# The RWKV stage of a decoder layer: elementwise work of POOL is given to DVE

## The chip, the cores and the metric

The kernel runs on one core of a Trainium2 chip. The metric is the device time of one execution in microseconds, as the median of several runs. Before the change it was 2909.91 us (three runs, 2908.15 to 2915.07).

The core's engines are named as the profile names them: PE (TensorE, matrix products; PEld is its weight load), DVE (VectorE), ACT (ScalarE), POOL (GpSimd) and SP (SyncE, which here issues the DMA transfers). Each works through its own queue in order and waits for the others by semaphores.

## The reference

One layer of a hybrid decoder, float32, on x of 1 x 1024 x 1024:

```
x <- x + 1/2 swiglu(rms_norm(x))
h  = rms_norm(x);  p = h @ w_in     -> RWKV columns | attention q, k, v | gates
y_a = rwkv7_time_mix(p_rwkv);  y_b = dilated_attention(q, k, v)
x <- x + (sigmoid(g_a) * (y_a @ w_proj_rwkv) + sigmoid(g_b) * (y_b @ w_proj_attn)) @ w_out
x <- x + 1/2 swiglu(rms_norm(x))
```

The part that matters here is the time mixing, with 16 heads of width 64:

```
r, k, v, ... = token_shift(p);  decay = exp(-exp(w));  a = sigmoid(...);  g = sigmoid(gd) @ g2
kk = heads(k * k_k);  kk = kk / max(sqrt(sum(kk * kk)), 1e-12)
k  = k * (1 + (a - 1) * k_a)
state_t = state * decay + (state @ -kk) (kk * a)^T + v k^T;   wkv_t = state_t @ r
y = (wkv - mean) * rsqrt(var + eps) * ln_w + ln_b
result = (y + sum(r * k * r_k) * v) * g
```

## The kernel before

All matrix products are float32 made of three products of high and low parts (`hi*hi + lo*hi + hi*lo`): ACT writes the high part, another engine subtracts it from the source to make the low part. The layer is a row of stages: a feed-forward half step, the attention with the projection of its columns, the RWKV stage with the rest of the projection, the output products, and a second half step.

The RWKV stage works on 8 pairs of heads (128 rows, `NP = 8`), each in two halves of 512 tokens: 16 units, numbered n. A half has 8 chunks (`HC`) of 64 tokens. For each unit four Python generators emit its instructions: `prep(n)` makes the decay products, kk, the scaled operands AL and BK and the masked chunk products Lab and MB; `solve(n)` inverts the triangular matrix of each chunk by five doubling steps (`pt` on PE, the masked B on DVE, `px` on PE, the sum XX and its transpose on DVE) and builds the chunk matrices M; `late(n)` transposes and makes the bonus; `chain(n)` carries the state SV through the 8 chunks and then normalises the output `o`, transposes it and writes y to the DRAM tensor `ya_d`.

Beside them runs the projection, `Dense.stream`: weight tiles of 128 columns, each loaded (`load`), split into `whi` and `wlo` (`parts`, lines 583 to 589) and multiplied by both halves of `hT` (`steps`, line 607, 24 products of 128x512 for a tile and a half of hT). Its products are what PE does while the solve waits. For a pair it makes k, r, v and mostly one gate tile. `db` is a second stream of that kind, for the attention's own projection with 768 rows, near the end of the stage.

The order comes from three layers. Each generator yields due times in units; `slotted` rounds those of the units down to sixteenths (`SLOTS = 16`); `drive` merges all generators by due time. That order is the priority with which the framework's scheduler then lays out each engine's queue, by its own costs of instructions, so that neighbours in a queue need not be neighbours in the code. In a queue the order is fixed. A tile pool with `bufs=n` hands a tag's buffer on when all uses of the tile that held it are done.

The lines that the change touches: line 588 (the low part of a weight tile: POOL where `pool_lo` is true, its default, which the attention stage uses as well), line 825 (`head_sum`: the low part `sl` for a sum over the rows of a head, called by `prep` for kk and by `late` for the bonus), lines 858 and 859 (the reciprocal of the root of kk, then its bound by 1e12), line 882 (r times the decay, the third part of AL), and lines 1096 to 1105 (the transposes of `o`, scale and shift by ln_w and ln_b on ACT out of PSUM, then bonus and gate on POOL). Others named later: L914 (`k2` times r_k and r, for the bonus), L669 (the carry of the token shift, one column), L876 (k's factor), L983, L985, L993 and L995 (B, the first XX, the later XX, the transpose of XX), L1048 to L1050 (M), L958 (the bonus itself, two buffers).

Of the kernel before, what the change touches and what calls it, by code (L numbers as in the profile page):

```python
# [9 lines left out]
AF = mybir.ActivationFunctionType  # L10
ALU = mybir.AluOpType
# [11 lines left out]
def f32(ap):  # L23
    return ap.bitcast(F32)
# [68 lines left out]
class Seven:  # L93
# [9 lines left out]
    def prep(self, j, n, k, lo, hi):  # L103

        nc, V = self.tc.nc, self.tc.nc.vector
        i = self.order[n]
        a11, a21, b11, b12 = lo
        a12, a22, b21, b22 = hi
        a, b = ((a11, b11), (a12, b21), (a11, b22), (a11, b11), (a21, b12), (a12, b22), (a22, b21))[i]
        ops = self.ring(j)  # L110
        split(nc, ops[0], ops[1], a)
        split(nc, ops[2], ops[3], b)
        self.b.append(ops)
        if i == 0:
            V.tensor_add(a21, a21, a22)
            V.tensor_sub(b12, b12, b11)
        elif i == 1:
            V.tensor_sub(a11, a21, a11)
            V.tensor_sub(a12, a12, a11)
        elif i == 5:  # L120
            V.tensor_sub(b22, b22, b12)
        elif i == 2:
            V.tensor_sub(a11, a22, a11)
            V.tensor_sub(b11, b22, b11)
        elif i == 3:
            V.tensor_sub(b21, b21, b22)
# [372 lines left out]
C = 64  # L499
# [67 lines left out]
class Dense:  # L567
# [15 lines left out]
    def parts(self, raw, n):  # L583
        nc, pool, kd = self.tc.nc, self.pool, self.kd
        whi = pool.tile([P, KD, P], F32R, tag="whi", name="whi", bufs=self.nw)
        wlo = pool.tile([P, KD, P], F32R, tag="wlo", name="wlo", bufs=self.nw)
        nc.scalar.copy(whi[:, :kd, :n], raw[:, :kd, :n])  # L587
        (nc.gpsimd if self.pool_lo else nc.vector).tensor_sub(wlo[:, :kd, :n], raw[:, :kd, :n], f32(whi[:, :kd, :n]))  # L588
        return whi, wlo

    def weights(self, c0, n=P):
# [84 lines left out]
SLOTS = 16  # L676
# [5 lines left out]
class Loras:  # L682
# [8 lines left out]
    def new(self, tag, shape, bufs=1, dt=F32):  # L691
        return self.pool.tile(shape, dt, tag="l_" + tag, name="l_" + tag, bufs=bufs)
# [92 lines left out]
class Rwkv:  # L785
# [34 lines left out]
    def head_sum(self, ps, src):  # L820

        nc, K = self.tc.nc, self.cx.K
        full, hi = src
        lo = self.new("sl", [P, HS], 1, F32R)
        nc.gpsimd.tensor_sub(lo, full, f32(hi))
        nc.tensor.matmul(ps, K["bones_r"], hi, start=True, stop=False)
        nc.tensor.matmul(ps, K["bones_r"], lo, start=False, stop=True)

    def prep(self, n):
        nc, cx, K, new = self.tc.nc, self.cx, self.cx.K, self.new  # L830
        p, half = n // 2, n % 2
        q, u = self.pairs[p], self.units[n]
        V, G = nc.vector, nc.gpsimd
        col = lambda name: K[name][:, p:p + 1]
        t0 = half * HS
        ts_ = slice(t0, t0 + HS)
        ch = lambda t: t.rearrange("p (c t) -> p c t", t=C)
        E, O = slice(0, 64), slice(64, 128)
        T = n - 2
        rows = slice(p * P, (p + 1) * P)  # L840
        at = lambda slot: T + slot / SLOTS
        yield at(-7)

        k = q.k[:, ts_]
        sq = new("sq", [P, HS])
        nc.scalar.activation(sq, k, AF.Square, scale=col("k_k"))
        hi = new("sh", [P, HS], 1, F32R)
        V.tensor_copy(hi, sq)
        pn = cx.ps_s.tile([P, 512], F32, tag="ps", name="pn")
        self.head_sum(pn, (sq, hi))  # L850
        kk = new("kk", [P, HS])
        nc.scalar.activation(kk, pn, AF.Sqrt)
        yield at(-6)
        tw, ta = new("tw", [P, HS]), new("ta", [P, HS])
        nc.sync.dma_start(tw, self.w_d[rows, ts_])
        nc.sync.dma_start(ta, self.a_d[rows, ts_])
        yield at(-4)
        V.reciprocal(kk, kk)
        G.tensor_scalar(kk, kk, 1e12, None, ALU.min)
        yield at(-3)  # L860
        V.tensor_tensor_scan(tw, K["reset"], tw, 0.0, ALU.mult, ALU.add)
        yield at(-1)
        lam = new("lam", [P, HC, C + 1])
        G.memset(lam[:, :, 0:1], 1.0)
        nc.scalar.activation(lam[:, :, 1:C + 1], ch(tw), AF.Exp, scale=-0.5 * E05)
        u.lamC = new("lamC", [P, HC, 1], 3)
        G.tensor_copy(u.lamC, lam[:, :, C:C + 1])
        nc.scalar.activation(tw, tw, AF.Exp, scale=0.5 * E05)
        inv = ch(tw)
        r = q.r[:, ts_]  # L870

        u.AL = AL = new("AL", [P, HC, 3, C], 2)
        yield at(1)
        V.scalar_tensor_tensor(kk, k, col("k_k"), kk, ALU.mult, ALU.mult)
        u.k2 = k2 = new("k2", [P, HS], 2)
        V.tensor_scalar(k2, ta, col("k_a"), col("c1"), ALU.mult, ALU.add)  # L876
        yield at(2)
        V.tensor_mul(k2, k2, k)
        V.tensor_mul(ta, ta, kk)
        BK = u.BK = new("BK", [P, HC, 2, C])  # L880
        yield at(4)
        G.tensor_mul(AL[:, :, 2], ch(r), lam[:, :, 1:C + 1])
        for b, h in enumerate((E, O)):
            yield at(4 + 2 * b)
            V.scalar_tensor_tensor(AL[h, :, b], ch(kk)[h], -1.0, lam[h, :, 0:C], ALU.mult, ALU.mult)
            V.tensor_mul(BK[h, :, b], ch(ta)[h], inv[h])
            yield at(5 + 2 * b)
            V.tensor_mul(BK[h, :, 1 - b], ch(k2)[h], inv[h])

        u.Lab = Lab = new("Lab", [P, HC, C], 2)  # L890
        u.MB = MB = new("MB", [P, HC, 2, P], 2)
        ms = lambda h: K["ms"][h].unsqueeze(1).broadcast_to([64, 4, C])

        def keep(x, base):
            G.affine_select(x, x, pattern=[[0, 4], [1, C]], compare_op=ALU.is_ge, fill=0.0, base=base, channel_multiplier=-1)
        for c0 in range(0, HC, 4):
            yield at(8 + c0 // 2)
            c4 = slice(c0, c0 + 4)
            heads = (E, O), (O, E)
            ps2 = [cx.ps_s.tile([P, 4, P], F32, tag="ps", name="plm") for _ in heads]  # L900
            for c in range(4):

                for e, (h, _) in enumerate(heads):
                    nc.tensor.matmul(ps2[e][:, c], BK[h, c0 + c].rearrange("p a b -> p (a b)"), AL[h, c0 + c, e:3:2 - e],
                                     start=True, stop=True)
            for e, (h, o) in enumerate(heads):
                ps = ps2[e]
                V.tensor_mul(Lab[h, c4], ps[h, :, 0:64], ms(h))
                nc.scalar.copy(AL[o, c4, e], ps[o, :, 0:64])
                nc.scalar.copy(MB[:, c4, e, self.TC[e]], ps[:, :, 64:128])  # L910
                keep(AL[o, c4, e], -1)
            if c0 == 0:
                yield at(9)
                V.scalar_tensor_tensor(k2, k2, col("r_k"), r, ALU.mult, ALU.mult)  # L914
        yield at(12)
        for e in range(2):
            for h in (E, O):
                for c0 in range(0, HC, 4):
                    keep(MB[h, c0:c0 + 4, e, self.TC[e]], 0)
# [132 lines left out]
    def chain(self, n):  # L1052
        nc, cx, K, new = self.tc.nc, self.cx, self.cx.K, self.new
        half = n % 2
        u = self.units[n]
        V = nc.vector
        yield n
        SV, lam = u.SV, u.lamC
        E, O = slice(0, 64), slice(64, 128)
        o = new("o", [P, 8, C])  # L1060
        for c in range(HC):
# [10 lines left out]
            if i == 3:  # L1072

                for par, dst in enumerate((E, O)):
                    for e, src in enumerate((O, E)):
                        k = slice(c - 3 + e, c + 1, 2)
# [3 lines left out]
        p = n // 2  # L1080
        col = lambda name: K[name][:, p:p + 1]
        ts_ = slice(half * HS, half * HS + HS)
        g = new("g", [P, HS])
        nc.sync.dma_start(g, self.g_d[p * P:(p + 1) * P, ts_])
        T = n + 1
# [7 lines left out]
        yield T + 0.20  # L1093
        V.reciprocal(st, st)
        V.tensor_mul(o, o, st.unsqueeze(2).broadcast_to([P, 8, C]))
        yield T + 0.27
        pt = cx.ps_s.tile([P, 4, P], F32, tag="ps", name="pyt")
        of = o.rearrange("p (i h) e -> p i (h e)", h=2)
        for c in range(4):
            nc.tensor.transpose(pt[:, c], of[:, c], cx.ident)  # L1100
        y = new("y", [P, HS])
        nc.scalar.activation(y, pt.rearrange("p a b -> p (a b)"), AF.Identity, bias=col("ln_b"), scale=col("ln_w"))
        yield T + 0.34
        nc.gpsimd.tensor_add(y, y, u.bonus)
        nc.gpsimd.tensor_mul(y, y, g)
        nc.sync.dma_start(self.y_d[p * P:(p + 1) * P, ts_], y)

    def run(self, gates, after):
# [335 lines left out]
def layer(tc, W, out):  # L1444
    nc = tc.nc
    cx = Ctx()
    with tc.tile_pool(name="const", bufs=1, reuse_waits="tile") as cp, tc.tile_pool(name="hT", bufs=1, reuse_waits="tile") as hp, \
# [3 lines left out]
        hT = fresh(F32R)  # L1451
# [24 lines left out]
        with ExitStack() as mix, ExitStack() as lt:  # L1476
# [70 lines left out]
            ps = lambda name, b: late.enter_context(pd(name, b))  # L1547
            cx.ps_s, cx.ps_c = ps("rs", 4), ps("rc", 2)
            rps = ExitStack()
            rw = Rwkv(tc, cx, dn, rps.enter_context(sb("rw")), rp2, dram, w_d, a_d, g_d, ya_d)  # L1550
            db = Dense(tc, cx, wp, hT, W["w_proj_attn"])

            def bring(t):
                yield t
# [22 lines left out]
            yp, y, w = None, [], []  # L1577
# [17 lines left out]
            wp = ws.enter_context(sb("w2"))  # L1595
# [6 lines left out]
        with os:  # L1602
# [4 lines left out]
            with ys, ws:  # L1607
# [6 lines left out]
                V = nc.vector  # L1614
# [125 lines left out]
```

## Time and profile before

| | before |
|---|---|
| median of three runs | 2909.91 us |
| the profiled execution | 2910.36 us, span 2908.6 us |
| PE busy | 2791.0 us, 96% |
| DVE busy | 2064.0 us, 71% |
| ACT busy | 1272.3 us, 44% |
| POOL busy | 738.9 us, 25% |
| RWKV stage | about 1140 to 2036 us of the span |

Busy time is the sum of an engine's instructions over the span. PE is busy nearly throughout; its products also take longer when the granted clock is low, so a busy PE need not be at its peak. The share of an engine over the whole span is an average over stages that have different limits.

### The profile page before, as it was taken

Reading aid. Unit: us, or ns where it says so; the run is one execution under the profiler, and the core shown is the slowest. Engines: PE = TensorE matmul, PEld = TensorE weight load, DVE = VectorE, ACT = ScalarE, POOL = GpSimd, SP = SyncE. Lnnn points to the kernel's source line nnn. Section 1 sums busy time; section 2 is a strip of 40 time slices with the busy share of each in tenths; the row PEclk is TensorE's granted clock in tenths of the full one; section 3 lists DMA queues with packets and bytes.
Section 4 is the critical chain, followed back from the end, with each engine's and each line's share of the span. In section 5 each row is a group of like instructions: output and inputs, shape, how many; then the busy total and the mean of one; then the engine's idle time right before and its main releaser. Section 6 shows DMA issues by size and latency. Waiting matters only on the chain. (4 is left out here: it accounts for less than half of the span.)

```text
span 2908.6 us, 56533 instructions
## 1 busy us (share of the span) xinstructions
PE 2791.0 (96%) x23406; PEld 2233.6 (77%) x23406; DVE 2064.0 (71%) x3058; ACT 1272.3 (44%) x2480; POOL 738.9 (25%) x739
## 2 busy tenths in 40 slices
PE   7999999998999999999999999999988999999999
PEld 5888887886667778777787777787767788887887
DVE  8666778997565763667666766624799777667998
ACT  5323332444566663455555556443435333233342
POOL 3332330001111112444343434322001333322000
PEclk9999999999999999999999999999999999999999
DMA  3222226103431123111111121128520122224221
GB/s 116 73 80 87 73 83 242 67 14 99 139 103 37 31 81 122 52 54 38 61 45 61 38 60 32 57 65 272 200 94 17 64 75 84 81 87 172 97 80 58
DMA packets 252242, 246.71 MB, mean 85 GB/s; under 512 B 26288, under 2 KB 192336, under 8 KB 251984
## 3 DMA queue, kind: packets, MB, share of 16 engines
q1 hardware_dynamic: 250832, 238.89, 25.2%
q8 instruction: 184, 3.01, 0.4%
q10 hardware_dynamic: 1152, 4.19, 0.4%
q14 instruction: 74, 0.61, 0.1%
HBM read 181.03 MB, written 62.01 MB: 84 GB/s over the span
## 5 line engine op out<-in xcount | busy, mean ns | idle before, releaser
L607 PE MATMUL pd<-hhi,whi 128*128 128x512 f32 (+1 forms) x1064 | 432.3, 406 | 5.2 <-DVE gb L1589 3.2
L607 PE MATMUL pd<-hlo,whi 128*128 128x512 f32 (+1 forms) x1064 | 436.1, 410 | 0.0
L607 PE MATMUL pd<-hhi,wlo 128*128 128x512 f32 (+1 forms) x1064 | 431.5, 406 | 0.6 <-POOL wlo L588 0.6
L282 PE MATMUL pp<-e,bh 128*128 128x512 f32 x1056 | 336.8, 399 | 3.9 <-ACT bh L74 2.3
L588 POOL TENSOR_TENSOR wlo<-raw,whi 128x1024 fp32r<-128x1024 f32 (+2 forms) x69 | 161.6, 2342 | 549.1 <-ACT whi L587 397.9
L282 PE MATMUL pp<-hhi,bl 128*128 128x512 f32 x704 | 276.4, 393 | 2.4 <-DVE bl L75 2.4
L282 PE MATMUL pp<-hhi,bh 128*128 128x512 f32 x704 | 277.3, 394 | 0.0
L282 PE MATMUL pp<-hlo,bh 128*128 128x512 f32 x704 | 276.1, 392 | 0.0
L74 ACT CAST bh<-rg 128x512 fp32r<-128x512 f32 x176 | 105.5, 621 | 344.4 <-DMA rg<-in_ffn_w_in_dram 172.3
L253 POOL TENSOR_TENSOR rg<-ru,rg 128x512 f32<-128x512 f32 x44 | 58.6, 1331 | 760.1 <-DVE bl L75 760.1
L607 PEld LDWEIGHTS pd<-hhi,whi 128*128 128x128 f32 (+1 forms) x1064 | 200.8, 189 | 52.4 <-issue 4.8
L282 PEld LDWEIGHTS pp<-e,bh 128*128 128x128 f32 x1056 | 200.0, 190 | 53.1 <-ACT bh L74 3.2
L607 PEld LDWEIGHTS pd<-hlo,whi 128*128 128x128 f32 (+1 forms) x1064 | 200.5, 188 | 48.0 <-issue 5.0
L607 PEld LDWEIGHTS pd<-hhi,wlo 128*128 128x128 f32 (+1 forms) x1064 | 200.9, 189 | 46.5 <-issue 4.8
L282 PE MATMUL pp<-e,bl 128*128 128x512 f32 x528 | 210.8, 399 | 0.0
L75 DVE TENSOR_TENSOR bl<-rg,bh 128x512 fp32r<-128x512 f32 x176 | 154.6, 879 | 73.8 <-ACT bh L74 73.8
L306 DVE TENSOR_TENSOR sg<-sg,pp 128x512 f32<-128x512 f32 x162 | 110.7, 683 | 102.3 <-PE pp L282 102.1
L282 PEld LDWEIGHTS pp<-hhi,bl 128*128 128x128 f32 x704 | 132.4, 188 | 33.3 <-DVE bl L75 3.3
L282 PEld LDWEIGHTS pp<-hlo,bh 128*128 128x128 f32 x704 | 132.3, 188 | 29.8
L282 PEld LDWEIGHTS pp<-hhi,bh 128*128 128x128 f32 x704 | 132.3, 188 | 29.3
L587 ACT CAST whi<-raw 128x1024 fp32r<-128x1024 f32 (+2 forms) x69 | 70.0, 1015 | 128.0 <-PE pd L607 72.0
L1071 ACT ACTIVATE SV<-pc,lamC 64x64 f32<-64x64 f32 x240 | 73.9, 308 | 113.8 <-PE pc L1068 111.6
(473 smaller groups left out, 6291.4 us busy)
## 6 DMA issues: line engine op xcount, KB each, us to landing
raw<-in_w_in_dram SPq DMA_DIRECT2D x60, 512.0 KB
rg<-in_ffn_w_in_dram SPq DMA_DIRECT2D x44, 512.0 KB
ru<-in_ffn_w_in_dram SPq DMA_DIRECT2D x44, 512.0 KB
act_d<-spill SPq DMA_DIRECT2D x80, 256.0 KB
e<-act_d SPq DMA_DIRECT2D x20, 512.0 KB
e<-in_ffn_w_out_dram SPq DMA_DIRECT2D x20, 512.0 KB
gt_d<-gate SPq DMA_DIRECT2D x32, 256.0 KB
x<-in_x_dram SPq DMA_DIRECT2D x8, 512.0 KB
```

Source lines behind the costliest of these rows:

```text
L74: nc.scalar.copy(hi, src)
L75: (eng or nc.vector).tensor_sub(lo, src, f32(hi))
L253: G.tensor_sub(b11, b12, b11)
L282: nc.tensor.matmul(ps, a[:, k], b[:, k], start=m == 0, stop=m == 11)
L306: add = lambda o, a: V.tensor_add(o, a, ps)
L587: nc.scalar.copy(whi[:, :kd, :n], raw[:, :kd, :n])
L588: (nc.gpsimd if self.pool_lo else nc.vector).tensor_sub(wlo[:, :kd, :n], raw[:, :kd, :n], f32(whi[:, :kd, :n]))
L607: nc.tensor.matmul(ps[:n], a[:, k, :n], b[:, k, t], start=i == 0, stop=i == 3 * kd - 1)
L1071: nc.scalar.activation(nxt[h, e], pc[h, i, e], AF.Copy, scale=lam[h, c])
```

## The change

DVE takes over POOL's work with two-dimensional tiles in the RWKV stage:

- The low part of a weight tile is made by DVE in pieces of four blocks of 128 columns (two for a tile) where `pool_lo` is false; that is set for the projection from the RWKV stage on, and for `db`.
- The rest `sl` of the sums over heads is made by DVE.
- kk is bounded from below by 1e-12 by DVE ahead of its reciprocal; before, the reciprocal was bounded from above by 1e12 by POOL.
- r times the decay is made by DVE.
- y: one DVE instruction takes the transposed output from PSUM, multiplies by ln_w and adds the bonus; a second adds ln_b and multiplies by the gate. ACT's instruction and POOL's two are gone. The transposes are due in slot 6 (before: 4), the last instruction in slot 7 (before: 5).

```
--- before.py
+++ after.py
@@ -585,7 +585,12 @@
         nc.scalar.copy(whi[:, :kd, :n], raw[:, :kd, :n])
-        (nc.gpsimd if self.pool_lo else nc.vector).tensor_sub(wlo[:, :kd, :n], raw[:, :kd, :n], f32(whi[:, :kd, :n]))
+        if self.pool_lo:
+            nc.gpsimd.tensor_sub(wlo[:, :kd, :n], raw[:, :kd, :n], f32(whi[:, :kd, :n]))
+        else:
+            for k in range(0, kd, 4):
+                k = slice(k, min(k + 4, kd))
+                nc.vector.tensor_sub(wlo[:, k, :n], raw[:, k, :n], f32(whi[:, k, :n]))
@@ -822,7 +827,7 @@
-        nc.gpsimd.tensor_sub(lo, full, f32(hi))
+        nc.vector.tensor_sub(lo, full, f32(hi))
@@ -855,8 +860,8 @@
         yield at(-4)
+        V.tensor_scalar(kk, kk, 1e-12, None, ALU.max)
         V.reciprocal(kk, kk)
-        G.tensor_scalar(kk, kk, 1e12, None, ALU.min)
@@ -879,7 +884,7 @@
         yield at(4)
-        G.tensor_mul(AL[:, :, 2], ch(r), lam[:, :, 1:C + 1])
+        V.tensor_mul(AL[:, :, 2], ch(r), lam[:, :, 1:C + 1])
@@ -1093,16 +1098,15 @@
-        yield T + 0.27
+        yield T + 6 / SLOTS
         pt = cx.ps_s.tile([P, 4, P], F32, tag="ps", name="pyt")
...
         y = new("y", [P, HS])
-        nc.scalar.activation(y, pt.rearrange("p a b -> p (a b)"), AF.Identity, bias=col("ln_b"), scale=col("ln_w"))
-        yield T + 0.34
-        nc.gpsimd.tensor_add(y, y, u.bonus)
-        nc.gpsimd.tensor_mul(y, y, g)
+        V.scalar_tensor_tensor(y, pt.rearrange("p a b -> p (a b)"), col("ln_w"), u.bonus, ALU.mult, ALU.add)
+        yield T + 7 / SLOTS
+        V.scalar_tensor_tensor(y, y, col("ln_b"), g, ALU.add, ALU.mult)
         nc.sync.dma_start(self.y_d[p * P:(p + 1) * P, ts_], y)
@@ -1547,8 +1551,9 @@
+            dn.pool_lo = False
             rw = Rwkv(tc, cx, dn, rps.enter_context(sb("rw")), rp2, dram, w_d, a_d, g_d, ya_d)
-            db = Dense(tc, cx, wp, hT, W["w_proj_attn"])
+            db = Dense(tc, cx, wp, hT, W["w_proj_attn"], pool_lo=False)
```

## Rows read from the trace of the kernel before

**Rows 1.** Windows: stretch, us, busy us of PE, PEld, DVE, ACT, POOL, clock, DMA.
```profile
1140.00:2036.00 896.00, 851.86 (x14748) 696.24 (x14747) 550.90 (x908) 458.26 (x1007) 354.71 (x475) 0.98 0.22 70
...
1326.00:1352.00 26.00, 20.95 (x580) 16.91 (x578) 20.45 (x34) 11.02 (x25) 7.49 (x6) 0.87 0.20 63
1426.00:1452.00 26.00, 21.68 (x597) 17.56 (x596) 21.48 (x37) 11.22 (x25) 7.49 (x6) 0.93 0.20 64
1525.00:1551.00 26.00, 21.66 (x596) 17.54 (x596) 21.29 (x37) 11.01 (x25) 7.49 (x6) 0.93 0.21 64
1623.00:1649.00 26.00, 20.56 (x596) 16.89 (x596) 21.43 (x37) 11.25 (x25) 7.48 (x6) 1.00 0.20 64
1721.00:1747.00 26.00, 21.79 (x592) 17.79 (x592) 21.06 (x35) 11.02 (x24) 7.48 (x6) 0.87 0.21 63
1819.00:1845.00 26.00, 22.53 (x586) 17.88 (x588) 17.63 (x30) 9.69 (x22) 7.04 (x11) 0.74 0.20 63
...
1367.00:1390.00 23.00, 22.92 (x379) 18.96 (x376) 17.32 (x33) 13.01 (x28) 5.51 (x8) 1.00 0.19 59
```

**Rows 2.** Waits in 1140 to 2036: total us, times, longest us.
```profile
PE pt L980 <- DVE XX L993: 15.6, 8, 2.3
PE px L991 <- DVE B L983: 7.6, 10, 1.2
PE pt L980 <- DVE M L1050: 5.8, 5, 1.2
...
DVE kk L874 <- POOL kk L859: 14.6, 15, 1.5
```

**Rows 3.** Timeline of DVE in an odd unit: start us, us, instruction.
```profile
1329.09 1.15 DVE L985 TENSOR_TENSOR XX<-B,eye 128x256 f32<-128x256 f32 x1
...
1335.26 2.75 DVE L914 SCALAR_TENSOR_TENSOR k<-k,v_r_k,r 128x512 f32<-128x512 f32 x1
...
1338.59 0.89 DVE L669 TENSOR_TENSOR r<-r,carry 128x1 f32<-128x1 f32 x1
1339.40 0.41 DVE L993 TENSOR_TENSOR XX<-XX,px 128x256 f32<-128x256 f32 x1
1339.73 1.36 DVE L876 TENSOR_SCALAR k<-ta,v_k_a,c 128x512 f32<-128x512 f32 x1
...
1343.05 0.41 DVE L983 TENSOR_TENSOR B<-pt,mk 128x256 f32<-128x256 f32 x1
```

**Rows 4.** Timeline of POOL in the same stretch, with its idle time before.
```profile
1328.78 1.19 POOL L882 TENSOR_TENSOR AL<-r,lam 128x512 f32<-128x512 f32 x1 [10.14 <-DVE M L1050]
...
1335.09 2.37 POOL L588 TENSOR_TENSOR wlo<-raw,whi 128x1024 fp32r<-128x1024 f32 x1 [1.18 <-ACT whi L587]
...
1339.54 1.26 POOL L1105 TENSOR_TENSOR y<-y,g 128x512 f32<-128x512 f32 x1
```

**Rows 5.** Single lines of code: count: ns least/median/most, first and last start.
```profile
L914 DVE SCALAR_TENSOR_TENSOR k<-k,v_r_k,r x16: 750/753/2748, 1155.5 to 1869.2; 128x512 f32<-128x512 f32 x16
...
L669 DVE TENSOR_TENSOR k<-k,carry x8: 148/150/153, 1150.7 to 1793.0; 128x1 f32<-128x1 f32 x8
...
L669 DVE TENSOR_TENSOR v<-v,carry x8: 1037/1047/1185, 1172.2 to 1861.6; 128x1 f32<-128x1 f32 x8
...
L876 DVE TENSOR_SCALAR k<-ta,v_k_a,c x16: 523/1182/1686, 1148.7 to 1827.5; 128x512 f32<-128x512 f32 x16
...
L75 DVE TENSOR_TENSOR ring<-y,ring x28: 678/688/708, 2029.6 to 2137.7; 128x512 fp32r<-128x512 f32 x28
```

**Rows 6.** Groups of POOL in 1140 to 2036: busy us, mean ns, idle before.
```profile
L588 POOL TENSOR_TENSOR wlo<-raw,whi 128x1024 fp32r<-128x1024 f32 (+1 forms) x43 | 99.1, 2305 | 95.4 <-ACT whi L587 77.9 <-PE pd L607 11.7 <-DVE gb L1589 5.7
```

**Rows 7.** Timeline of an even unit: DVE's first XX, PE's use of it.
```profile
1376.07 0.41 DVE L985 TENSOR_TENSOR XX<-B,eye 128x256 f32<-128x256 f32 x1
...
1377.69 0.75 PE L980 MATMUL pt<-XX,Lab 32*32 32x32 f32 x64
```

## The prediction

> **What bounds the kernel now.** I read the page first: TensorE is the busiest engine by far, so a change is worth only what it takes out of TensorE's idle time and out of its slow-clock time. The edits touch one stage, the RWKV stage, so next came the windows of that stage. In them the reader is to see [rows 1] that in 896 us TensorE is busy 851.9, idle 44.1, at a mean granted clock of 0.98. DVE is busy 551 us, 61%, POOL 355: by the average DVE is far from a bound. The windows by stretch show that the loss is local. In six stretches of 26 us, one in nearly every pair of heads, TensorE idles 5.05, 4.32, 4.34, 5.44, 4.21 and 3.47 us, 26.8 together, and there the granted clock falls to 0.87, 0.93, 0.93, 1.00, 0.87 and 0.74: weighted by length 17.2 us, an upper bound of what the low level (1.2 in place of 2.4 GHz) costs. The stretch between two of them (1367 to 1390) has TensorE busy 22.92 of 23 us. I call the units with a loss odd, the others even.
>
> Third, the waits of TensorE [rows 2]: it waits for DVE, in the triangular solve. `pt` waits for the sum XX (8 times, 15.6 us, longest 2.3), `px` for the masked B (10 times, 7.6), the first `pt` of a unit for the adds of M (5 times, 5.8). A separate row is DVE's own wait for POOL at kk, 14.6 us over 15 times.
>
> Fourth, the DVE queue inside one of the stretches [rows 3], beside POOL's [rows 4]. DVE is full there, and some of its instructions are far too long: L985 takes 1.15 us, 0.41 in an even unit [rows 7]; L914 2.75 against a median of 0.753 [rows 5]; L669, one column, 0.89 against 0.15 [rows 5]; L876 1.36 against 0.523 at best [rows 5]. Each of these runs while POOL works: L882 from 1328.78 to 1329.97, L588 from 1335.09 to 1337.46, L1105 from 1339.54 to 1340.80. L914 starts 0.17 after L588 and ends at 1338.01, 0.55 after it: it stood until POOL was done. L993, which reads PSUM and one SBUF tile, runs 0.41 us at its usual length. So POOL's three large instructions hold up the DVE queue on which TensorE's solve waits.
>
> **The change part by part.** POOL loses its two-input work in this stage: 43 low parts of weight tiles [rows 6] (2305 ns each), two rests for the head sums per unit, r times the decay, the bound on kk, the bonus and the gate. Affine selects, copies and memsets stay. DVE gets, per unit of 16: per weight tile two subtractions of 128x512, nearest row 0.688 us [rows 5], so 1.38 (2.7 tiles per unit: 3.7 us); two rests at the same 0.69; r at 0.69; two fused adds and multiplies for y, nearest row L914's median, 0.75 each; one maximum, not in the trace in this form: bounds 0.15 (L669) and 0.75, I take 0.52 as L876's best. Together 7.8 us a unit, 125 us in all; DVE would go from 551 towards 676 of 896 us, less what it no longer stands still. ACT loses 16 activations of y, which are off the path.
>
> *In an odd unit, up to XX.* Of the queue ahead of L993 at 1339.40 [rows 3], L985 gives back 1.15 - 0.41 = 0.74, L914 2.75 - 0.75 = 2.00, L669 0.89 - 0.15 = 0.74: 3.48 us. What enters: r (0.69, its place is before the AL products) and one low part (1.38, it is ready at 1335, just where L914 stands). Net 3.48 - 2.07 = 1.41 earlier. TensorE's wait of 2.3 becomes 0.9. If the low part is queued behind L993 instead, it is 2.8 earlier and the wait is gone; if a rest and a y instruction come ahead too, it is nothing (-1.41 + 1.44). I take 1.41.
>
> *From XX to the next B.* L876 gives back 1.36 - 0.52 = 0.84. B at 1343.05 then comes 2.25 earlier, while TensorE arrives 1.41 earlier: a wait for B at that place (up to 1.2 by rows 2) shrinks by 0.84. The bound from the other side is 0, if y or a rest takes that place. The y instructions move from slots 4 and 5 to 6 and 7, which is behind this stretch, so I take 0.84. Six stretches times 2.25 is 13.5 us.
>
> *What stays.* The wait for M (some 1.15 each) lies ahead of POOL's first instruction in the stretch, and the first B comes from six products in a row: nothing is removed there, I count 0.
>
> *The clock.* If half of the idle time in the stretches goes, I take half of the 17.2 us, 8.6; bounds 0 and 17.2. The row for it: the stretch at 1623 idles most, 5.44, and has clock 1.00, so idle time alone doesn't fix the loss [rows 1].
>
> The Trainium skill, in "TensorE: Matmul & The Clock Gate", section "HAM oscillation — how this bites in real kernels", tells of a loop whose repeated idle gaps throw the clock back to half rate in every round. Five of the six stretches agree with it, the one at 1623 does not. By that rule the waits that remain would go on costing the whole 17.2, and the sum would be 8.6 us less; this is a rival below.
>
> *In an even unit.* DVE's XX at 1376.07 ends at 1376.48, TensorE takes it at 1377.69 [rows 7]: 1.21 us to spare. A low part (1.38) and r (0.69) come ahead of it, the one-column L669 there gives back 1.05 - 0.15 = 0.90 [rows 5]: 1.17 later, just hidden. If the cover is gone, 0.7 each in seven units, 5 us; if the low part falls elsewhere, nothing. I take 1 us.
>
> *kk.* The 14.6 us that DVE waits for POOL go, and the maximum adds some 0.5 a unit. Neither stands where TensorE waits: 0, bounds -2 and +1. What is late next there is nothing that TensorE waits for, since its even stretches are full.
>
> *y and bonus.* The transposes of y stand two slots later and y is now read from PSUM by DVE. The bonus tile has two buffers; the bonus of the unit after next is due in slot 5, while the old one is now read in slot 6, so its product waits for y and its PSUM bank is held a slot longer (3.1 us). Behind it on DVE stand XX or B of the solve. I count 0; bounds 0 and 1 us a unit, 14 us, the nearest row being a wait for B, 0.76 on average [rows 2].
>
> *DMA.* No transfer is added. y's store is issued from SP up to two slots later (a unit is half of the 100 us from one stretch to the next, a slot a sixteenth of it, 3.1 us); its reader is a whole stage away save for the last unit. 0.
>
> Sum: -13.5 - 8.6 + 1 = -21 us. The profiled execution took 2910.4 us (span 2908.6); the median of the three runs is 2909.9, 0.5 below it, which is nothing here. The forecast is 2889 us.
>
> **The rivals.**
> *DVE becomes the bound (slower).* Place: the even units, between the last add of M and XX. Price: if half of a unit's 7.8 us lands there, 3.9 - 0.9 given back - 1.21 to spare is 1.8 a unit, 14 us in eight; odd units then gain almost nothing (3.9 against 4.3 given back), and a clock loss as in the odd ones (17.2 / 6 = 2.9) in one unit of three adds 8. 2910 + 22 = 2932. It decides from the point where the first XX in an even unit comes more than 1.21 us later. For it: 7.8 us a unit is much, and the queue is in order. Against it: most of it (rests, maximum, y) belongs to slots where DVE idles.
> *The gap is refilled (no change).* In odd units a rest and a y instruction take the place of the stalls: 4.3 given back, 2.07 + 0.69 + 1.5 put in. About 2908. Against it: y's new slots.
> *The clock stays low.* Idle time falls as forecast but 17.2 stays: 2889 + 8.6 = 2898.
> *Everything goes.* With no POOL in the way the order of the queue works out as planned, and the six stretches lose all 26.8 and 17.2: 2866. Against it: the waits for M and first B.
> That the change does not do what it says I hold for unlikely: the flag is set before the stage's first tile is split.
>
> **How the numbers follow.** Forecast 0.42 (its own range 2880 to 2898), clock stays 0.15, everything goes 0.12, no change 0.15, DVE the bound 0.16. The first three are faster by over 0.3% (8.7 us, about what a measurement of this kernel can tell from no change): 0.69; same 0.15; slower 0.16. The range goes from 2864, just under the case in which everything goes, to 2914, past no change; what is left out is most of the slower case.
>
> **What would show it.** In the profile after: L914, L985, L669 and L876 at their short lengths; POOL below 150 us in the stage; DVE near 600 to 630 us; the wait of `pt` for L993 falling from 15.6 to some 6 us, that for M staying near 5.8; in the stretches idle time near 3 us and a clock above 0.93. I am wrong if the stretches keep their 26.8 us, if the even stretches show idle time, or if `pt` or `px` wait for a DVE queue in which new subtractions or y stand just ahead of XX or B.

## The result, and the profile after

The changed kernel takes 2875.52 us (median of four runs, 2873.60 to 2878.34) against 2909.03 for the kernel before in the same comparison (four runs, 2907.44 to 2915.07): the ratio is 0.9882, with a 95% interval of 0.9865 to 0.9899. It is 33.5 us faster, where 21 were forecast. The profiled span falls from 2908.6 to 2872.4 us.

Lines of code shift: L588, L669, L876, L914, L983, L985, L993 and L1050 of before are L593 (on DVE), L674, L881, L919, L988, L990, L998 and L1055 of after.

Up to 1140 us the two profiles agree (TensorE busy 1101.35 and 1101.10 us), and the part behind the stage is only 2.0 us shorter (859.9 and 857.9). The difference lies in the RWKV stage, taken here from 1140 to the end of its last dense product. First windows of the kernel before that are not in [rows 1] (stretch, length, busy us of PE, PEld, DVE, ACT, POOL, clock, DMA), then those of after, the six stretches among them:

```profile
1140.00:2048.70 908.70, 864.55 (x14804) 706.75 (x14803) 557.57 (x918) 458.26 (x1007) 354.71 (x475) 0.98 0.23 74
...
1170.00:1200.00 30.00, 25.94 (x431) 20.11 (x431) 22.08 (x31) 13.53 (x26) 14.12 (x20) 0.94 0.19 64
...
1960.00:2048.50 88.50, 82.10 (x395) 66.88 (x394) 38.16 (x56) 29.53 (x58) 17.98 (x11) 0.98 0.80 268
```

```profile
1140.00:2014.50 874.50, 853.65 (x14804) 698.10 (x14803) 607.52 (x1099) 448.42 (x991) 142.64 (x335) 1.00 0.24 77
...
1170.00:1200.00 30.00, 29.11 (x570) 22.96 (x570) 24.96 (x42) 13.59 (x26) 6.28 (x16) 1.00 0.29 90
...
1320.00:1346.00 26.00, 23.89 (x693) 19.30 (x694) 22.79 (x48) 13.71 (x30) 2.92 (x8) 1.00 0.21 64
1415.00:1441.00 26.00, 23.89 (x688) 19.20 (x688) 22.79 (x48) 13.70 (x30) 2.84 (x8) 1.00 0.20 64
1510.00:1536.00 26.00, 23.77 (x672) 18.93 (x670) 22.71 (x48) 13.61 (x30) 2.68 (x8) 1.00 0.20 64
1605.00:1631.00 26.00, 23.95 (x672) 19.05 (x671) 22.59 (x47) 13.49 (x31) 2.41 (x7) 1.00 0.21 64
1701.00:1727.00 26.00, 22.62 (x664) 18.17 (x665) 21.27 (x45) 12.11 (x29) 1.62 (x5) 1.00 0.21 65
1795.00:1821.00 26.00, 23.92 (x642) 19.32 (x643) 21.92 (x38) 14.68 (x35) 8.30 (x19) 1.00 0.21 64
...
1930.00:2014.40 84.40, 80.40 (x383) 65.00 (x382) 46.22 (x74) 25.92 (x53) 0.00 (x0) 0.98 0.83 278
```

The stage is 34.2 us shorter. TensorE's idle time (length less busy) falls from 44.15 to 20.85, by 23.3 us; its busy time falls by 10.9 at the same number of products, which is the clock. The six stretches lose 12.9 us of idle time (26.8 to 13.96) and all of them are at clock 1.00. So 10.4 us of idle time go elsewhere: from 1170 to the first stretch 6.6 become 1.6 (the rows at 1170: 4.06 and 0.89), between the last two stretches 3.2 become 0.6, and at the end of the stage 6.4 become 4.0.

The waits of TensorE in the stage of after, up to 2002 us (total, times, longest), to be set beside [rows 2]:

```profile
PE pt L985 <- DVE M L1055: 5.8, 5, 1.2
PE px L996 <- issue: 2.7, 5, 0.7
...
PE pt L985 <- DVE XX L998: 2.5, 7, 0.4
...
PE px L996 <- DVE B L988: 1.2, 2, 0.8
...
PE pt L985 <- DVE XX L990: 0.4, 1, 0.4
```

The waits for XX and B, 15.6 and 7.6 before, are 2.5 and 1.2. The wait for M is 5.8 in both. The wait for the first XX of a unit (L990) was 5.5 us, three times, before, and is 0.4. DVE's queue in the odd unit: first the line of before from which the stretch is counted, then after (start, us, instruction), for [rows 3]:

```profile
1328.63 0.42 DVE L983 TENSOR_TENSOR B<-pt,mk 128x256 f32<-128x256 f32 x1
```

```profile
1322.46 0.42 DVE L988 TENSOR_TENSOR B<-pt,mk 128x256 f32<-128x256 f32 x1
...
1322.99 0.42 DVE L990 TENSOR_TENSOR XX<-B,eye 128x256 f32<-128x256 f32 x1
...
1328.09 0.42 DVE L988 TENSOR_TENSOR B<-pt,mk 128x256 f32<-128x256 f32 x1
...
1329.26 0.69 DVE L593 TENSOR_TENSOR wlo<-raw,whi 128x512 fp32r<-128x512 f32 x1
...
1330.53 0.15 DVE L674 TENSOR_TENSOR r<-r,carry 128x1 f32<-128x1 f32 x1
1330.60 0.42 DVE L998 TENSOR_TENSOR XX<-XX,px 128x256 f32<-128x256 f32 x1
1330.93 0.75 DVE L919 SCALAR_TENSOR_TENSOR k<-k,v_r_k,r 128x512 f32<-128x512 f32 x1
...
1331.95 0.65 DVE L593 TENSOR_TENSOR wlo<-raw,whi 128x512 fp32r<-128x512 f32 x1
...
1336.05 0.71 DVE L1107 SCALAR_TENSOR_TENSOR y<-pyt,v_ln_w,bonus 128x512 f32<-128x512 f32 x1
```

Every instruction shown has its short length. From the first B to the XX that TensorE waits for, DVE took 10.8 us (1328.63 to 1339.40) and now takes 8.1 (1322.46 to 1330.60). One piece of the low part stands ahead of XX; L919 and the second piece are behind it.

### The profile page after: what moved, and what is told of

Read it like the earlier page. It is cut to its first block, busy times and chain, and to the rows that moved or that the text cites. A ratio compares the mean times of both kernels' runs of the same rounds, so it can differ in the third digit from the quotient of the medians.

```text
span 2872.4 us, 56514 instructions
## 1 busy us (share of the span) xinstructions
PE 2780.8 (97%) x23406; PEld 2226.0 (77%) x23406; DVE 2114.0 (74%) x3242; ACT 1261.6 (44%) x2464; POOL 522.4 (18%) x599
## 4 chain that ended last, share of the span: by engine, by line
PE 78%; DVE 14%; ACT 3%; issue 2%; DMA 2%; SPq 0%; DVEq 0%; ACTq 0%
PE pp L282 26%; PE pd L612 23%; PE pp L139 2%; PE pp L140 2%; PE pp L138 2%; PE po L140 2%; PE po L138 2%; PE po L139 2%; PE pt L985 2%; PE pc L1073 1%; PE pl L777 1%; PE pz L1031 1%; PE px L996 1%; PE po L373 1%; PE plm L909 1%
## 5 line engine op out<-in xcount | busy, mean ns | idle before, releaser
L253 POOL TENSOR_TENSOR rg<-ru,rg 128x512 f32<-128x512 f32 x44 | 58.3, 1326 | 842.6 <-DVE bl L75 842.6
L282 PEld LDWEIGHTS pp<-hhi,bl 128*128 128x128 f32 x704 | 132.8, 189 | 33.5 <-DVE bl L75 3.3
L589 POOL TENSOR_TENSOR wlo<-raw,whi 128x1024 fp32r<-128x1024 f32 (+1 forms) x25 | 60.0, 2401 | 444.9 <-ACT whi L587 412.5
```

The source lines that it names most:

```text
L253: G.tensor_sub(b11, b12, b11)
L282: nc.tensor.matmul(ps, a[:, k], b[:, k], start=m == 0, stop=m == 11)
L589: nc.gpsimd.tensor_sub(wlo[:, :kd, :n], raw[:, :kd, :n], f32(whi[:, :kd, :n]))
```

## The experiments

Three theories stood at the start. A: POOL's reads of SBUF hold DVE's instructions, and taking the work from POOL frees them. B: the order of the queues does it, above all the new slots of y. C: neither part is worth much without the others. Times are medians, with the ratio to the kernel before (2908.05 to 2910.01 in these comparisons) and its interval.

**Parts alone.** wlo_only, only the low parts of the weight tiles on DVE (with the lines of `parts` as in the change):

```
...
+            dn.pool_lo = False
...
-            db = Dense(tc, cx, wp, hT, W["w_proj_attn"])
+            db = Dense(tc, cx, wp, hT, W["w_proj_attn"], pool_lo=False)
```

> The kernel before with only the low parts of the weight tiles on DVE. Theory A (POOL's reads hold DVE): L914 is short again (0.75), L669 and L876 in part stay long, because r, y and the rests are still on POOL; DVE gets 59 us more. About 1 us a stretch is gained: 2895 to 2905 us. Theory C (the parts only work together, since each stall that goes leaves the next one in the same queue): within 5 us of before.

Measured: 2901.06, 0.9969 [0.9958, 0.9980], in A's range and outside C's. TensorE's waits for XX (L998) become 14.7 us, those for B 12.5, which were 15.6 and 7.6: what the shorter L914 frees is lost again at B.

small_only, only the rests of the head sums, kk's bound and r on DVE:

```
-        nc.gpsimd.tensor_sub(lo, full, f32(hi))
+        nc.vector.tensor_sub(lo, full, f32(hi))
...
+        V.tensor_scalar(kk, kk, 1e-12, None, ALU.max)
         V.reciprocal(kk, kk)
-        G.tensor_scalar(kk, kk, 1e12, None, ALU.min)
...
-        G.tensor_mul(AL[:, :, 2], ch(r), lam[:, :, 1:C + 1])
+        V.tensor_mul(AL[:, :, 2], ch(r), lam[:, :, 1:C + 1])
```

> The kernel before with only the rests, the bound of kk and r on DVE. Theory A: L985 is short again (0.41), L914 stays long behind the low part; the wait of pt for XX stays near 2 us each: 2898 to 2908 us. Theory C: within 5 us of before.

Measured: 2898.79, 0.9963 [0.9948, 0.9978], in A's range and outside C's. The first XX takes 419 ns on average, L914 still 1407.

y_only, only the edit of y (engines and slots), and y_slots, only y's slots, its work left on ACT and POOL:

```
-        yield T + 0.27
+        yield T + 6 / SLOTS
...
-        yield T + 0.34
+        yield T + 7 / SLOTS
```

> The kernel before with only the edit of y: transposes in slot 6, two instructions of DVE in the place of one of ACT and two of POOL. Theory A: only L876 and L669 are freed, 1.6 us a stretch: 2895 to 2903 us. Theory C: within 5 us of before, since L914 holds the queue ahead of XX.

> The kernel before with the transposes of y in slot 6 and its last part in slot 7, but on ACT and POOL as before: no instruction changes its engine. Theory B (order): what the edit of y gains comes from the place of the transposes, so the same time as the run with the edit of y alone, 2 us or less between them. Theory A: POOL's two instructions now hold other DVE instructions, so no gain: 2905 to 2912 us.

Measured: y_only 2893.14, 0.9943 [0.9928, 0.9957]; y_slots 2892.06, 0.9937 [0.9921, 0.9954]. y_only is a little faster than A had expected. y_slots is what B had expected: the slots alone bring all of it, and the engine of y nothing that can be measured. A had forecast no gain here, because no work leaves POOL; that falls. The trace of y_slots shows how the slots work. POOL's queue there, then DVE's, in the unit of [rows 3, 4]:

```profile
1337.13 2.37 POOL L588 TENSOR_TENSOR wlo<-raw,whi 128x1024 fp32r<-128x1024 f32 x1 [1.18 <-ACT whi L587]
...
1346.56 1.27 POOL L1104 TENSOR_TENSOR y<-y,bonus 128x512 f32<-128x512 f32 x1 [0.87 <-ACT y L1102]
```

```profile
1337.29 2.75 DVE L914 SCALAR_TENSOR_TENSOR k<-k,v_r_k,r 128x512 f32<-128x512 f32 x1
...
1340.62 0.14 DVE L669 TENSOR_TENSOR r<-r,carry 128x1 f32<-128x1 f32 x1
1340.69 0.41 DVE L993 TENSOR_TENSOR XX<-XX,px 128x256 f32<-128x256 f32 x1
1341.02 0.53 DVE L876 TENSOR_SCALAR k<-ta,v_k_a,c 128x512 f32<-128x512 f32 x1
...
1342.94 0.39 DVE L983 TENSOR_TENSOR B<-pt,mk 128x256 f32<-128x256 f32 x1
1343.26 0.67 DVE L878 TENSOR_TENSOR k<-k,k 128x512 f32<-128x512 f32 x1
```

L914 stands beside L588 as before. But y has left 1338 to 1341 for 1346, and L669 and L876 are short. The order helps too: L878 is now behind B. From XX to B it is 2.25 us, where it was 3.65 [rows 3]: 0.83 from L876 and most of the rest from L878. So in this trace the slots gain both by order (B) and because a read of POOL is moved away in time (A's mechanism); no run separates the two.

no_wlo (the whole change without the low parts) and no_y (without the edit of y):

> The kernel after with the low parts of the weight tiles back on POOL (rests, bound, r and y stay on DVE). Theory A: L588 held L914 for 2.0 of the 3.5 us that were freed ahead of XX, so more than half of the gain goes: 2890 to 2905 us, L919 long again. Theory B: most of the gain stays, 2875 to 2885 us. If DVE's own load is what limits now, this is faster than after: under 2872 us.

> The kernel after with y as before: the transposes in slot 4, scale on ACT, bonus and gate on POOL. Theory A: only L881 is held again (0.84 us in an odd unit) and L674 in part: 2880 to 2888 us. Theory B (the moved transposes of y changed the order around the third pt): half of the gain goes, 2890 us or more.

Measured: no_wlo 2891.97, 0.9950 [0.9932, 0.9969], in A's range; no_y 2892.78, 0.9944 [0.9929, 0.9959], which is what B had forecast and not A. In no_y the instructions that A had named are all short (means of L881 538 ns, L919 749, r's L674 148), and still TensorE's waits for XX (L998) are 11.4 us, where after has 2.5. In the odd unit y's two steps on POOL stand beside other instructions of DVE (DVE, then POOL):

```profile
1332.82 1.41 DVE L593 TENSOR_TENSOR wlo<-raw,whi 128x512 fp32r<-128x512 f32 x1
...
1334.48 1.95 DVE L866 TENSOR_TENSOR_SCAN tw<-reset,tw 128x512 f32<-128x512 f32 x1
```

```profile
1332.24 1.43 POOL L1109 TENSOR_TENSOR y<-y,bonus 128x512 f32<-128x512 f32 x1 [3.69 <-ACT y L1107]
1333.75 1.60 POOL L1110 TENSOR_TENSOR y<-y,g 128x512 f32<-128x512 f32 x1
```

In after these two take 0.65 and 1.22 us. So the reads that are left on POOL lengthen what now stands beside them, and a price from the instructions of the old queue alone misses that.

Alone, the low parts bring 9.0 us, the small ones 11.2 and the slots 18.0: each is worth something without the others, so C falls as it was put. But the parts do not simply add up, though 38.2 together lies near the 33.5 of the whole. The small ones with the edit of y (no_wlo) bring 17 us, no more than that edit alone; the low parts bring 9.0 alone and 16.5 on top of the other two.

What each gives back is not the same thing. The windows of the stage, to the end of its last dense product, of wlo_only and of small_only (one profiled execution each):

```profile
1140.00:2040.30 900.30, 855.36 (x14813) 698.15 (x14813) 586.87 (x1005) 459.03 (x1009) 267.20 (x431) 1.00 0.24 74
```

```profile
1140.00:2041.20 901.20, 865.67 (x14820) 707.40 (x14819) 567.50 (x983) 461.17 (x1009) 280.14 (x411) 0.98 0.24 75
```

| stage in | idle us | busy us |
|---|---|---|
| before | 44.15 | 864.55 |
| wlo_only | 44.94 | 855.36 |
| small_only | 35.53 | 865.67 |
| y_slots | 33.51 | 859.19 |
| no_wlo | 30.16 | 858.54 |
| no_y | 33.32 | 856.58 |
| after | 20.85 | 853.65 |

In these executions wlo_only saves no idle time at all; it gives back 9.2 us of clock. small_only saves 8.6 us of idle time and no clock. For the clock this is less sure than for the idle time: the granted clock of a whole execution is 0.986 to 0.990 in the ten of before in this comparison, 0.990 to 0.992 in the seven of wlo_only and 0.987 to 0.991 in the four of small_only, of which the profiled one is the lowest.

**Reads put back on POOL.** dummy_read leaves the changed kernel as it is and lets POOL do the low parts and r a second time, into a tile that nothing reads:

```
+                nc.gpsimd.tensor_sub(junk[:, :m, :n], raw[:, k, :n], f32(whi[:, k, :n]))
                 nc.vector.tensor_sub(wlo[:, k, :n], raw[:, k, :n], f32(whi[:, k, :n]))
...
+        G.tensor_mul(junk.rearrange("p a b -> p (a b)").rearrange("p (c t) -> p c t", t=C), ch(r), lam[:, :, 1:C + 1])
         V.tensor_mul(AL[:, :, 2], ch(r), lam[:, :, 1:C + 1])
```

> The kernel after, in which POOL once more subtracts the high part from each weight tile and multiplies r by the decay, as before, but into a scratch tile that nobody reads; PE's queue is the same as after's, DVE's differs in a few places near the end of the stage. Theory A (POOL's reading instructions hold DVE's instructions, and so the solve on which PE waits): L919, L990, L674 and L881 grow long again, PE's idle time in the RWKV stage goes from 21 us back to 40 or more, the clock falls again in some stretches, and the time is 2900 to 2930 us, since DVE now has the moved work besides. Theory B (the gain comes from the new order of the queues): the order is the same, so 2875 to 2880 us.

Measured: 2892.60, 0.9942 [0.9928, 0.9957]; TensorE's queue is that of after, and DVE's nearly so. It loses 17 of the 33.5 us: A in direction, but less than the range that I had stated (2900 to 2930); B alone falls too. TensorE's idle time in the stage (1140 to 2029.5) is 34.66 us, 13.8 more than in after, and the waits for XX are 13.3 more (16.2 for 2.9), so the loss lies where A has it. The clock did not fall (busy 854.84 us). The rests, kk's bound and y are not put back here, so for the other 16 us reads and order are not told apart. In the odd unit, DVE and then POOL:

```profile
1333.41 1.65 DVE L596 TENSOR_TENSOR wlo<-raw,whi 128x512 fp32r<-128x512 f32 x1
...
1335.65 0.56 DVE L677 TENSOR_TENSOR r<-r,carry 128x1 f32<-128x1 f32 x1
1336.13 0.41 DVE L1003 TENSOR_TENSOR XX<-XX,px 128x256 f32<-128x256 f32 x1
```

```profile
1333.08 3.12 POOL L595 TENSOR_TENSOR junk<-raw,whi 128x512 f32<-128x512 f32 x2 [1.25 <-ACT whi L587]
```

Both DVE instructions beside POOL's reads are long again, 1.65 in place of 0.69 and 0.56 in place of 0.15, and the wait of `pt` for XX is 13.3 us.

dummy_write has fills of that tile in place of the reads, at both places:

```
+                for _ in range(2):
+                    nc.gpsimd.memset(junk, 0.0)
```

> The kernel after, in which POOL fills a scratch tile with zeros at the same places and for about as long (two fills of 128x512 for each half of a weight tile, two for r); the queues of PE and DVE are the same as after's. Theory A, with POOL's reads as the cause: fills read nothing, L919 keeps 0.75 us, 2875 to 2880 us. Theory A, with POOL's being busy at all as the cause: as with the subtractions, 2900 us or more. Theory B: 2875 to 2880 us. Told apart from B only together with the run that reads.

Measured: 2896.58, 0.9955 [0.9940, 0.9970], outside all its ranges: the fills, without an input, did not run at the intended places but from early in the stage, and TensorE waited 13.4 us for POOL's copies of W. So it says nothing on the theories. dummy_write2 ties each pair of fills to its place by a one-column copy of ACT into the tile:

```
+                nc.scalar.copy(junk[:, 0, 0:1], f32(whi[:, k.start, 0:1]))
+                for _ in range(2):
+                    nc.gpsimd.memset(junk, 0.0)
```

> The kernel after, in which POOL fills a scratch tile with zeros for about as long as it subtracted before (two fills of 128x512 for each half of a weight tile, two for r); a one-column copy of ACT ahead of each pair ties the fills to the time at which the subtractions were due, which the fills without it were not. PE's queue is that of after. If what holds DVE is POOL's reading: DVE's instructions keep their short lengths and the time is 2875 to 2882 us. If it is POOL's being busy: L593, L990 and L674 grow as in the run that reads, 2888 us or more.

Measured: 2883.20, 0.9908 [0.9886, 0.9930]. The lengths on DVE from 1140 to 2002 us (count, busy us, mean ns, idle before):

```profile
L597 DVE TENSOR_TENSOR wlo<-raw,whi 128x512 fp32r<-128x512 f32 x75 | 51.0, 698 | 26.5 <-ACT whi L587 26.3
L927 DVE SCALAR_TENSOR_TENSOR k<-k,v_r_k,r 128x512 f32<-128x512 f32 x16 | 12.0, 749 | 0.3
...
L678 DVE TENSOR_TENSOR r<-r,carry 128x1 f32<-128x1 f32 x8 | 1.2, 148 | 0.0
```

They are those of after (698, 749, 148), with POOL busy 251 us in the stage, where dummy_read has 286; with the reads the first and last were 918 and 456. The time misses the forecast range (2875 to 2882) by a little and stays well below that of the reads. So reads of POOL hold these DVE instructions and its writes don't. The Trainium skill has this rule in "SBUF — State Buffer", section "Who interferes with whom": a DVE instruction with two inputs in SBUF contends with a POOL instruction that reads SBUF, not with one that only writes. This trace agrees (918 and 698 ns above). That sentence does not cover L876, which has one tile as its input and was long beside POOL as well (1.36 us, [rows 3]). The 7.7 us by which dummy_write2 stays behind after come with other waits (`pm` for an ACT copy, 3.4 us in six); I haven't settled them.

**Beyond the change.** attn_too makes the low parts on DVE in the attention stage as well:

```
-            dn = Dense(tc, cx, wp, hT, W["w_in"])
+            dn = Dense(tc, cx, wp, hT, W["w_in"], pool_lo=False)
```

> The kernel after with the low parts of the weight tiles on DVE in the attention stage as well. If POOL's reads cost time wherever DVE's queue feeds PE, a few us more are gained: 2868 to 2873 us. If they cost only where DVE is full, as in the odd stretches (in the attention stage DVE is busy 60 to 68%, PE 96 to 99%), nothing: 2873 to 2879 us; DVE's 26 tiles more, 36 us, can also make it slower.

Measured: 2865.00 (2864.11 to 2871.16), 0.9852 [0.9832, 0.9872]: the fastest version by its median, and below the range that either theory had given. The ratio's interval overlaps a little with that of after. Each of its four executions is below every one of bonus3 and y_late below (2872.88 or more), which were taken beside it and are no faster than after. The profiled execution is its slowest, and its span (2869.4) is only 3 us shorter than after's. The attention stage, in after and in attn_too:

```profile
690.00:1140.00 450.00, 438.79 (x2168) 326.57 (x2167) 270.65 (x365) 262.48 (x507) 65.01 (x37) 0.99 0.28 87
```

```profile
690.00:1140.00 450.00, 444.13 (x2204) 332.36 (x2203) 288.54 (x421) 262.41 (x509) 8.70 (x18) 0.99 0.29 91
```

TensorE's idle time there falls from 11.2 to 5.9 us; its wait for the tile a_nm (in the attention) goes from 2.2 to 0.5. Whether POOL's reads were behind that wait was not tested, and the rest of the 10 us by which the medians differ is not explained.

bonus3 gives the bonus three buffers (the first of these edits alone), y_late has those and puts y into slots 8 and 9:

```
-        u.bonus = new("bonus", [P, HS], 2)
+        u.bonus = new("bonus", [P, HS], 3)
...
-        yield T + 6 / SLOTS
+        yield T + 8 / SLOTS
...
-        yield T + 7 / SLOTS
+        yield T + 9 / SLOTS
```

> The kernel after with three buffers of the bonus in the place of two, so that its product need not wait for the y that reads the old one. If that wait costs, as one of the costs that the prediction counted at nothing, 2 to 10 us are gained: 2865 to 2873 us. If it is hidden, 2873 to 2878 us.

> The kernel after with three buffers of the bonus, the transposes of y in slot 8 and its last part in slot 9. In after the first y stands just ahead of B (L988) and px then waits 0.5 to 0.7 us in five stretches: with y later these 3 us go, 2870 to 2874 us. If the order matters in other ways, slower than with three buffers alone.

Measured: bonus3 2876.68, 0.9887 [0.9869, 0.9905]; y_late 2877.35, 0.9889 [0.9868, 0.9910]; neither is apart from after's 0.9882. A wait for the bonus tile, which the prediction named under y and counted at 0, costs nothing that can be measured, and y_late misses its range: slots still later gain nothing.

## Why the prediction was right, and where it was mis-sized

- *POOL's instructions hold DVE's queue*: right. L919, L990, r's L674 and L881 have their short lengths (means 749, 420, 148 and 542 ns), POOL is busy 143 us in the stage, DVE 608; dummy_read and dummy_write2 show that the reads do it. One reading was off: L669 (1338.59 to 1339.48) stood beside a fourth instruction of POOL, the first step of y, and not beside L1105:

```profile
1338.20 1.26 POOL L1104 TENSOR_TENSOR y<-y,bonus 128x512 f32<-128x512 f32 x1 [0.74 <-ACT y L1102]
```

  k's one-column add (L674) did not stay short: its median goes from 150 ns before to 341. One instance, at 1305.89, stands beside a select that POOL keeps (1305.82, 0.41 us) and ends with it.
- *The six stretches, 13.5 us of idle time*: measured 12.9. That the sums lie so close is partly luck, for the parts are shifted: I let a whole low part (1.38) enter ahead of XX and kept L914 there, but only one piece (0.69) entered and L919 (0.75) went behind, so the wait of 2.3 us became 0.37 and not 0.9. Against that stand waits of TensorE that I had at nothing: in five stretches `px` waits 0.3 to 0.7 for nothing that the trace shows (2.7 us together), in one `pt` 1.1.
- *L669's and L876's returns* stand in the sum under POOL's removed work. y_slots shows that they come from moving y two slots, whoever does it: there L876 has a median of 546 ns and r's L669 of 143, with POOL's reads of y still made.
- *The step that failed* is the rest of the stage. 44.1 us of idle time stood in [rows 1], and I followed the 26.8 in the six stretches and gave the other 17.3 nothing. They lost 10.4. The sentence on kk, "Neither stands where TensorE waits: 0", is false in one of the first units. DVE's queue there in the kernel before, with the instruction of the last pair in which L985 was longest, and then TensorE's two waits:

```profile
1182.48 0.88 DVE L874 SCALAR_TENSOR_TENSOR kk<-k,v_k_k,kk 128x512 f32<-128x512 f32 x1 [1.38 <-POOL kk L859]
1183.39 0.42 DVE L983 TENSOR_TENSOR B<-pt,mk 128x256 f32<-128x256 f32 x1
1183.73 0.91 DVE L878 TENSOR_TENSOR k<-k,k 128x512 f32<-128x512 f32 x1
1184.57 0.41 DVE L985 TENSOR_TENSOR XX<-B,eye 128x256 f32<-128x256 f32 x1
...
1817.58 2.55 DVE L985 TENSOR_TENSOR XX<-B,eye 128x256 f32<-128x256 f32 x1
```

```profile
1185.13 1.08 PE L980 MATMUL pt<-XX,Lab 32*32 32x32 f32 x64 [2.52 <-DVE XX L985]
...
1820.19 1.08 PE L980 MATMUL pt<-XX,Lab 32*32 32x32 f32 x64 [2.63 <-DVE XX L985]
```

  DVE stood 1.38 us for POOL's kk right ahead of a B and an XX, and TensorE waited 2.52 us for that XX. At 1817.58 a first XX was held for 2.55 us, and TensorE waited 2.63. Both were in the trace, as a wait for L985 of 5.5 us in three; 1.4 us of the second lie ahead of the stretch that begins at 1819. In after 0.4 is left of the 5.5. small_only, with kk's bound on DVE, leaves 0.4 of the first and 2.0 of the second; wlo_only leaves 2.5 of the first and 0.5 of the second. A wait at the stage's end for the tile gb (3.2 us, 1.3 after) went as well, with a changed order there, and so did 2.9 of the 3.3 us that TensorE waited for B and later XX from 1230 to 1326 and from 1747 to 1819.
- *The clock, 8.6 us*: 10.9 by the busy time, between the bounds. The basis was wrong, though: I tied it to half of the idle time, and wlo_only gives back 9.2 us at the idle time of before. The rival "the clock stays low" did not come about: 2.1 to 3.4 us of idle time remain in each stretch, at clock 1.00. The Trainium skill, in "TensorE: Matmul & The Clock Gate", section "HAM oscillation — how this bites in real kernels", tells of a loop in which the wait of every round throws the clock back. wlo_only does not agree: its stage has 44.94 us of idle time, with waits for XX of up to 2.3 us as before, at clock 1.00.
- *M and the first B, 0*: the wait for M is 5.8 us, as forecast. *Even units, +1*: not seen; 1346 to 1415 idles 0.15 us of 69, and *DVE the bound* fell with it. (The 0.7 a unit of its upper bound is not worked out in the prediction.) *y and bonus, 0* for their new places: right, by y_late and bonus3.

The profiled spans lie 36.2 us apart, 15.2 more than the forecast of 21: 10.4 of idle time outside the stretches, 2.3 of clock, 2.0 behind the stage, 1.0 of even units that cost nothing, less 0.6 in the stretches. The time lies in the forecast range, below the likeliest case's own (2880 to 2898), and above "everything goes" (2866): 20.85 us of idle time stay.

Open: whether the M wait of 5.8 us can go (not tried), how the gain divides between POOL's reads and the order of the queues, and what set the clock. TensorE's busy time in the stage is 854 to 857 us in after, no_y, wlo_only, dummy_read and dummy_write2, which have the low parts on DVE, and 858 to 866 in the versions that have them on POOL; dummy_write, with waits of up to 9.0 us for W, has them on DVE and is at 861.9.

## What to carry to other kernels

A long instruction in a queue that feeds TensorE is to be read beside what POOL does at that moment. A read by POOL can be removed, or moved to another slot, and two slots for one step, with the new order that they brought, were worth 18 us here. A read that stays on POOL can lengthen another instruction once the queues have shifted. When waits are priced, add up the idle time of the whole stage and account for what lies outside the pattern that was found first. The clock's part did not follow the sum of the idle time here, so it needs a row of its own.

## What the runs showed of the hardware

POOL's reads lengthen even a one-column DVE instruction: 0.15 us became 0.89 in the kernel before and 0.56 in dummy_read; beside fills of POOL it took 0.15 (dummy_write2). TensorE's granted clock was 1.00 in the stage of wlo_only with 44.9 us of idle time and the same longest wait for XX (2.3 us) as before, where the stage had 44.15 at 0.98. These are single executions.
